# Convolution taps dealt out on VectorE's queue over retention, keys and attention, and probabilities scaled on ScalarE

## The chip, the cores and the metric

The kernel runs on one core of one Trainium2 chip. The metric is the device time of one execution in microseconds (us), from the first to the last instruction and what lies around them. A core has the engines TensorE (PE: matrix products, with a queue of its own for loading weights, PEld), VectorE (DVE), ScalarE (ACT), GpSimd (POOL) and SyncE (SP, which issues the DMAs here). Each engine works through its own queue in order.

## What is computed

A transformer block of two layers on 512 tokens of width 1024 in float32. The normed input is projected once (`w_in`), and its columns feed three branches: attention over compressed, selected and windowed keys with 8 heads in 2 groups, retention with 4 heads, and a convolution module. The branches are projected, mixed by sigmoid gates and added; a feed-forward with a squared ReLU follows. What the change touches:

```python
def _masked_softmax(s, mask):
    s = jnp.where(mask, s, -1e30)
    m = jnp.max(s, axis=-1, keepdims=True)
    p = jnp.exp(s - m) * mask
    den = jnp.sum(p, axis=-1, keepdims=True)
    return p / jnp.maximum(den, 1e-30)

def _conv_module(a, b, dw_w, dw_b, ln_g, ln_b):
    u = a * jax.nn.sigmoid(b)
    kern = dw_w[:, None, :].astype(u.dtype)
    y = lax.conv_general_dilated(u, kern, window_strides=(1,), padding=[(CONV_WIDTH - 1, 0)],
                                 dimension_numbers=('NWC', 'WIO', 'NWC'), feature_group_count=CONV_CH)
    y = y + dw_b
    y = _layernorm(y, ln_g, ln_b)
    return jax.nn.silu(y).astype(a.dtype)
...
        gs = jax.nn.sigmoid(gb.astype(jnp.float32)).reshape(B, Q_BLOCK, G, HPG, 3)
        o = gs[..., 0:1] * o_c + gs[..., 1:2] * o_s + gs[..., 2:3] * o_w
```

The convolution is depthwise: 512 channels, 31 taps each, over the tokens.

## The kernel before

Every product of two matrices is made in three: each operand is split into a high part and the remainder, and the products high by high, high by low and low by high are added up in PSUM (`proj`, L156). Weights are streamed from HBM by SP into `wr` (three buffers); ACT makes the high part `wh` (L144), POOL the low part `wl` in two halves (L147; in the feed-forward DVE does, L149). Activations are split by `split` (L110): ACT copies the high part (L111), DVE subtracts (L112). Tokens lie along the free axis, 512 wide, channels along the 128 partitions, so most tiles are 128x512.

A scheduler orders each engine's queue by a simulated timeline of its own: of the instructions whose inputs it takes to be there it puts the first in program order. `tc.issue_after(i)` adds one constraint: what is written inside it stands behind instruction `i` on `i`'s engine.

A layer runs like this. The normed input X is split (`norm_split`). `conv_input` (L303) makes one of four blocks of 128 channels of the convolution's input `u`, the first ahead of the retention, the others after its heads. The depthwise convolution is 31 taps for each of 4 channel blocks, 124 in a layer; each is one DVE instruction on 128x512 (the first of a block L331, the others L333) that multiplies a shifted view of `u` by a column of weights and adds it into `yc`. They stand in a list `todo`, and `conv_taps(n)` (L324) writes the next `n` where it is called, if their `u` has been written. It is called with 2 after each of 8 rotations (`T_ROT`, L362), with 1 after each of 16 score splits of the retention (`T_SCORE`, L418), with 2 after each of 64 pieces in attention (`T_QUERY`, L722), and for the rest at L748. As nothing holds a tap back but its input and the tap before it, those taps that are called for in retention suffice, with what the scheduler pulls forward, to place all 124 ahead of the first query.

The retention of a head computes scores on PE, multiplies them by the decay on DVE (L416), splits them (L111, L112) and forms the product with the values in the PSUM tile `av` (L108 is every product's line). Then the keys follow: `compress` (L481) lays blocks of tokens out (`XP`, L496) and projects them to the compressed keys and values; other projections are split into the attention's keys (L558) and values (L567), and the first query is projected (`query`, L636; its DVE step `tq` is L641).

Attention has 16 blocks in a layer: 4 turns `j`, 2 groups `g`, 2 branches `br`, each of one head. A block: scores of 4 pieces of 128, 256, 384 and 512 columns in the PSUM tile `sc`, bias and maximum on DVE (L705), exponential and denominator on ACT (L706), the gate over the denominator (`gate_over`, L617, three small DVE operations), and then for each piece

```python
nc.vector.tensor_scalar(cols[i], cols[i], c[:, i:i + 1], None, op0=OP.mult)
pt = ps("tp")
for k in range(i + 1):
    nc.tensor.transpose(pt[:, k * P:(k + 1) * P], cols[i][:, k * P:(k + 1) * P], ident)
```

(L712 to L715), the split of the transposed piece by ACT (L720) and DVE (L721), and at the block's end eight products with the values into `av`. PE's order interleaves this with fillers, pieces of work that are ready long before: the projection of the retention's output mixed with a gate, and gates ahead of time (`fill`, L470; their DVE step is `g`, L444). 19 of 24 fillers are dealt over the 16 blocks, each behind the first score product of a block (L743, L744); the others come after attention. Once all taps are written, `conv_norm` (L578) normalises the convolution in four steps between the blocks. PSUM has 3 banks for `mm`, 2 for `sc`, 2 for `tp` and 1 for `av`.

## Time and profile before

| | |
|---|---|
| runs of the kernel before | 1836.65, 1838.71, 1839.05 us (median 1838.71) |
| the profiled execution | 1835.35 us |
| its span, first to last instruction | 1833.6 us |
| mean granted TensorE clock over the span | 0.983 |

The page of the profile gives each engine's busy time over the span, which averages over stages with different limits. The span in slices and tables of stretches show the stages apart: retention and keys, attention, mixing and feed-forward, twice. Lines of waits say which engine waited for which tile, and how long; groups by shape give one instruction's mean time. The granted clock is the share of full speed at which TensorE was let run.

### The profile page before, as it was taken

The numbers are of one execution on the slowest core, as the hardware profiler recorded it, in microseconds if no ns is written. First come the engines' busy times: TensorE is split into PE (matmuls) and PEld (weight loads), VectorE is DVE, ScalarE is ACT, GpSimd is POOL, SyncE is SP. The second block draws the span as 40 slices with busy tenths as digits, with TensorE's granted clock in tenths as the row PEclk, the third lists the DMA queues.
The fourth block names the chain that finished last, engine by engine and source line by source line (L and its number), as shares of the span: only waits on it lengthen the run. The fifth ranks groups of instructions, "written<-read, shape, count | busy, mean of one in ns | idle before, by whom it ended". The sixth has DMA issues, their size and how long they took to land.

```text
span 1833.6 us, 23278 instructions
## 1 busy us (share of the span) xinstructions
PE 1759.7 (96%) x8592; PEld 1474.4 (80%) x8592; DVE 1162.1 (63%) x2107; ACT 721.4 (39%) x1293; POOL 512.0 (28%) x420
## 2 busy tenths in 40 slices
PE   8899899999999999999999878999999999999997
PEld 7777788888888888888897767888888888888886
DVE  7999977777554343434479998767766443434344
ACT  4423445566343232323433324555653432313231
POOL 4444433423471000000344544343235700000000
PEclk9999999999999999999999989999999999999998
DMA  4221442322653223233422113233128432232221
GB/s 165 83 74 59 130 150 94 113 87 81 229 167 104 92 92 103 92 94 102 144 81 75 65 58 129 98 110 109 69 81 268 141 97 92 93 103 92 94 91 69
DMA packets 70801, 195.82 MB, mean 107 GB/s; under 512 B 8944, under 2 KB 9328, under 8 KB 70688
## 3 DMA queue, kind: packets, MB, share of 16 engines
q1 hardware_dynamic: 70688, 194.34, 32.2%
q8 instruction: 68, 1.11, 0.2%
q14 instruction: 45, 0.37, 0.1%
HBM read 177.51 MB, written 19.42 MB: 107 GB/s over the span
## 4 chain that ended last, share of the span: by engine, by line
PE 58%; issue 21%; DVE 20%; DMA 1%; ACT 0%; SPq 0%; POOLq 0%; POOL 0%; DVEq 0%; ACTq 0%
PE mm L108 50%; DVE yc L333 9%; PE sc L108 3%; PE av L108 2%; PE tp L715 2%; DVE pr L112 1%; PE tp L108 1%; DVE rt L416 1%; DVE kv L558 1%; DVE qk L381 1%; DVE rr L359 0%; DVE t L395 0%; DVE XP L496 0%; DMA m<-in_cmp_w_k_dram 0%; DVE rr L360 0%
## 5 line engine op out<-in xcount | busy, mean ns | idle before, releaser
L108 PE MATMUL mm<-X,wh 128*128 128x512 f32 x2432 | 772.8, 396 | 17.4 <-ACT X L213 6.2
L147 POOL TENSOR_TENSOR wl<-wr,wh 128x512 fp32r<-128x512 f32 (+2 forms) x344 | 442.2, 1308 | 530.4 <-ACT wh L144 478.9
L144 ACT ACTIVATE wh<-wr 128x1024 fp32r<-128x1024 f32 (+2 forms) x301 | 296.4, 986 | 658.7 <-PE mm L108 554.1
L108 PEld LDWEIGHTS mm<-X,wh 128*128 128x128 f32 x2432 | 455.1, 190 | 108.3 <-ACT X L213 6.2
L108 PE MATMUL mm<-X,wl 128*128 128x512 f32 x1216 | 480.7, 395 | 0.2 <-DVE wl L149 0.2
L108 PEld LDWEIGHTS mm<-X,wl 128*128 128x128 f32 x1216 | 230.6, 190 | 46.8 <-DVE wl L149 0.6
L333 DVE SCALAR_TENSOR_TENSOR yc<-u,ccol,yc 128x512 f32<-128x512 f32 x240 | 227.5, 960 | 1.9
L149 DVE TENSOR_TENSOR wl<-wr,wh 128x1024 fp32r<-128x1024 f32 x129 | 158.1, 1225 | 38.6 <-ACT wh L144 38.6
L108 PE MATMUL mm<-bo,wh 128*128 128x512 f32 x512 | 163.5, 397 | 6.3 <-DVE g L444 5.8
L108 PE MATMUL mm<-fa,wh 128*128 128x512 f32 x512 | 160.2, 395 | 0.0
L796 DVE SCALAR_TENSOR_TENSOR t<-mm,rs 128x512 f32<-128x512 f32 x64 | 43.9, 691 | 161.3 <-PE mm L108 156.0
L205 POOL TENSOR_TENSOR n<-n,mhalf 128x4 f32<-128x4 f32 x15 | 18.1, 1208 | 403.8 <-DVE n L203 403.8
L226 POOL TENSOR_TENSOR t<-t,t 128x512 f32<-128x512 f32 x18 | 27.4, 1524 | 333.6 <-DVE wl L149 314.4
L108 PE MATMUL mm<-kv,wh 128*128 128x512 f32 x384 | 119.5, 389 | 0.0
L108 PEld LDWEIGHTS mm<-bo,wh 128*128 128x128 f32 x512 | 97.5, 191 | 26.8 <-DVE g L444 6.2
L108 PEld LDWEIGHTS mm<-fa,wh 128*128 128x128 f32 x512 | 96.1, 188 | 23.2
L721 DVE TENSOR_TENSOR pt<-tp,pt 128x256 fp32r<-128x256 f32 (+1 forms) x192 | 70.3, 373 | 55.2 <-ACT pt L720 54.7
L108 PE MATMUL mm<-bo,wl 128*128 128x512 f32 x256 | 101.2, 395 | 0.0
L108 PE MATMUL mm<-fa,wl 128*128 128x512 f32 x256 | 100.6, 395 | 0.0
L108 PE MATMUL mm<-wh,X 128*128 128x256 f32 (+1 forms) x480 | 94.5, 295 | 4.2 <-DVE t L307 4.2
L720 ACT ACTIVATE pt<-tp 128x256 fp32r<-128x256 f32 (+1 forms) x192 | 63.9, 343 | 86.0 <-PE tp L715 53.3
L807 DVE TENSOR_TENSOR yc<-yc,mm 128x512 f32<-128x512 f32 x32 | 22.0, 688 | 105.6 <-PE mm L108 105.6
(219 smaller groups left out, 2449.2 us busy)
## 6 DMA issues: line engine op xcount, KB each, us to landing
wr<-in_w_dram SPq DMA_DIRECT2D x128, 512.0 KB, 3.5
wr<-in_w_f_dram SPq DMA_DIRECT2D x87, 512.0 KB, 3.2
wr<-in_w_b_dram SPq DMA_DIRECT2D x48, 256.0 KB, 2.7
wr<-in_w_t_dram SPq DMA_DIRECT2D x16, 512.0 KB, 3.2
gd<-g SPq DMA_DIRECT2D x32, 256.0 KB, 2.0
g<-gd SPq DMA_DIRECT2D x32, 256.0 KB, 3.3
wr<-in_w_o_dram SPq DMA_DIRECT2D x16, 512.0 KB, 3.6
md<-g SPq DMA_DIRECT2D x16, 256.0 KB, 2.6
```

Of the source, the lines that this page charges most:

```text
L108: return nc.tensor.matmul(o, l, r, start=start, stop=stop)
L112: (eng or nc.vector).tensor_sub(lo, src, f(hi))
L144: nc.scalar.activation(h, t, AF.Copy)
L147: nc.gpsimd.tensor_sub(l[:, k], t[:, k], f(h[:, k]))
L149: nc.vector.tensor_sub(l, t, f(h))
L226: (nc.vector if c == KC - 1 or first_time else nc.gpsimd).tensor_add(s, s, acc)
L333: nc.vector.scalar_tensor_tensor(yc[c], x, w, yc[c], op0=OP.mult, op1=OP.add)
L715: nc.tensor.transpose(pt[:, k * P:(k + 1) * P], cols[i][:, k * P:(k + 1) * P], ident)
L720: nc.scalar.activation(vh, src, AF.Copy)
L721: nc.vector.tensor_sub(vl, src, f(vh))
L796: nc.vector.scalar_tensor_tensor(t, pf, 0.0, rs, op0=OP.max, op1=OP.mult)
L807: nc.vector.tensor_add(xT[m], xT[m], pf)
```

## The change

The two calls that deal taps in the retention are given other numbers (1 after each rotation, 2 after each score split), and new ones stand in the keys (3 after each of the 4 layings-out of L496 and after each of the 2 key splits, 6 after the values). Whatever is then left of `todo` is counted (`late_taps`) and dealt evenly over the first 52 of attention's 64 pieces. Each call is now `conv_taps_behind`, which puts the taps on DVE's queue behind the operation that it follows, so that the scheduler no longer takes them forward. For that, `split` returns its subtraction. The scaling of the probabilities by the gate over the denominator, 128 instructions in all, goes from DVE to ACT, as a copy with a scale of one value per partition.

```diff
--- before.py
+++ after.py
@@ -74,7 +74,8 @@
     count = [0]
 
 
-    T_ROT, T_SCORE, T_QUERY = 2, 1, 2
+
+    T_ROT, T_SCORE, T_KEYS, T_SLOTS = 1, 2, 3, 52
 
 
     AHEAD, F_KEYS, HELD = 16, 1, 4
@@ -109,7 +110,7 @@
 
     def split(hi, lo, src, eng=None):
         nc.scalar.activation(hi, src, AF.Copy)
-        (eng or nc.vector).tensor_sub(lo, src, f(hi))
+        return (eng or nc.vector).tensor_sub(lo, src, f(hi))
 
     def halves(g):
 
@@ -315,6 +316,10 @@
             nc.gpsimd.memset(u[:, :CW - 1], 0.0)
             nc.vector.scalar_tensor_tensor(u[:, CW - 1:], tb, 1.0, ta, op0=OP.add, op1=OP.mult)
             us.append(u)
+
+        def conv_taps_behind(ins, n):
+            with tc.issue_after(ins.ins):
+                conv_taps(n)
 
         conv_input(0)
         yc = [tl(cp, "yc", 4) for _ in range(4)]
@@ -357,9 +362,9 @@
                 nc.vector.tensor_mul(B[:, :, 0, :], z[:, :, 1, :], sinb)
                 nc.vector.tensor_mul(B[:, :, 1, :], z[:, :, 0, :], sinb)
                 nc.vector.tensor_sub(A[:, :, 0, :], A[:, :, 0, :], B[:, :, 0, :])
-                nc.vector.tensor_add(A[:, :, 1, :], A[:, :, 1, :], B[:, :, 1, :])
+                rotated = nc.vector.tensor_add(A[:, :, 1, :], A[:, :, 1, :], B[:, :, 1, :])
                 rr.append(A)
-                conv_taps(T_ROT)
+                conv_taps_behind(rotated, T_ROT)
             for c in range(2):
                 pt = ps("tp")
                 for i in range(NB):
@@ -414,8 +419,7 @@
                 mm(s[:, :n], KSr[h][:, j * P:(j + 1) * P], QLr[h][:, j * P:], False, True)
                 t = tl(rp, "rt", 2)
                 nc.vector.tensor_mul(t[:, :n], s[:, :n], dec[:, :n])
-                split(ph[:, at[j]], pl[:, at[j]], t[:, :n])
-                conv_taps(T_SCORE)
+                conv_taps_behind(split(ph[:, at[j]], pl[:, at[j]], t[:, :n]), T_SCORE)
             o = ps("av")
             for j in range(NB):
                 mm(o[:, j * P:], VHr[j][:, h % 2, :], ph[:, at[j]], j == 0, False)
@@ -493,7 +497,8 @@
             pe = par(pe_at, 16)
             for g in range(2):
                 blocks = bass.AP(tensor=E.tensor, offset=E.offset + g * T, ap=[list(E.ap[0]), [2, 16], [16, NCMP]])
-                nc.vector.tensor_add(XP[:, :, g, :], blocks, pe[:, :, None].to_broadcast([P, 16, NCMP]))
+                laid = nc.vector.tensor_add(XP[:, :, g, :], blocks, pe[:, :, None].to_broadcast([P, 16, NCMP]))
+                conv_taps_behind(laid, T_KEYS)
             w1t = []
             for u in range(2):
                 t = tl(rp, "w1", 4, (P, 8, P))
@@ -555,7 +560,8 @@
                 nc.scalar.activation(KHH[br, g][nat], t[nat], AF.Copy)
                 nc.scalar.activation(KHH[br, g][oth], t[nat], AF.Copy)
                 for half in (nat, oth):
-                    nc.vector.tensor_sub(KLL[br, g][half], t[nat], f(KHH[br, g][nat]))
+                    low = nc.vector.tensor_sub(KLL[br, g][half], t[nat], f(KHH[br, g][nat]))
+            conv_taps_behind(low, T_KEYS)
         G = tl(mix_pool, "G", 1, (P, NB, 24))
         V = []
         pz = [ps(tag) for tag in ("mm", "mm", "mm", "av")]
@@ -564,10 +570,11 @@
             v = kv((P, 4, P))
             zv = pz[i][:, :256].rearrange("p (c d) -> p c d", d=DH)
             nc.scalar.activation(v[:, :, 0:64], zv, AF.Copy, scale=rs4[:, i:i + 1])
-            nc.vector.scalar_tensor_tensor(v[:, :, 64:128], zv, rs4[:, i:i + 1], f(v[:, :, 0:64]), op0=OP.mult,
-                                           op1=OP.subtract)
+            low = nc.vector.scalar_tensor_tensor(v[:, :, 64:128], zv, rs4[:, i:i + 1], f(v[:, :, 0:64]), op0=OP.mult,
+                                                 op1=OP.subtract)
             nc.scalar.activation(G[:, i, :], pz[i][:, 256:280], AF.Tanh, scale=rs4h[:, i:i + 1])
             V.append(v)
+        conv_taps_behind(low, 2 * T_KEYS)
         phase.close()
 
         def ut(dtype=F):
@@ -709,7 +716,7 @@
                     c = gate_over(den, h, 1 + br)
                     ph, pl = tl(ap, "pt", 4, (P, 1280), FR), tl(ap, "pt", 4, (P, 1280), FR)
                     for i in range(NB):
-                        nc.vector.tensor_scalar(cols[i], cols[i], c[:, i:i + 1], None, op0=OP.mult)
+                        nc.scalar.activation(cols[i], cols[i], AF.Copy, scale=c[:, i:i + 1])
                         pt = ps("tp")
                         for k in range(i + 1):
                             nc.tensor.transpose(pt[:, k * P:(k + 1) * P], cols[i][:, k * P:(k + 1) * P], ident)
@@ -718,8 +725,9 @@
                             if len(vh.shape) == 3:
                                 src = src.rearrange("p (k q) -> p k q", q=P)
                             nc.scalar.activation(vh, src, AF.Copy)
-                            nc.vector.tensor_sub(vl, src, f(vh))
-                        conv_taps(T_QUERY)
+                            low = nc.vector.tensor_sub(vl, src, f(vh))
+                        slot = 4 * (4 * j + 2 * g + br) + i
+                        conv_taps_behind(low, late_taps * (slot + 1) // T_SLOTS - late_taps * slot // T_SLOTS)
                     for k, c0 in enumerate((0, 512, 896, 1152)):
                         n = T - k * P
                         lhs = V[k][:, 2 * br + g, :]
@@ -732,6 +740,7 @@
             return oj
 
         ON, marks, tqs = [], [], [query(0)]
+        late_taps = len(todo)
 
         def more(j, k):
```

What this does to the queues is shown at three places of layer 0. Names are those of the tiles with a running number; `yc` is a sum of the convolution, `u` its input, L333 before is L338 now, L112 is L113, and L721 is L728.

On DVE's queue, at the end of the first retention head's scores and in the convolution input that follows (`rt` decayed scores, `pr` their low part, `t` and `u` of the input, `n` small sums), there stood before

```order
L112 TENSOR_TENSOR pr_817<-rt_837,pr_816 128x256
L333 SCALAR_TENSOR_TENSOR yc_260<-u_257,ccol,yc_260 128x512
L112 TENSOR_TENSOR pr_817<-rt_845,pr_816 128x128
L333 SCALAR_TENSOR_TENSOR yc_260<-u_257,ccol,yc_260 128x512 x5
L307 TENSOR_TENSOR t_920<-mm_888,rs_179 128x512
L313 TENSOR_TENSOR t_954<-mm_887,rs_179 128x512
L333 SCALAR_TENSOR_TENSOR yc_260<-u_257,ccol,yc_260 128x512
L316 SCALAR_TENSOR_TENSOR u_956<-t_920,t_954 128x512
L333 SCALAR_TENSOR_TENSOR yc_260<-u_257,ccol,yc_260 128x512
L331 TENSOR_SCALAR yc_261<-u_956,ccol,pcol 128x512
L333 SCALAR_TENSOR_TENSOR yc_261<-u_956,ccol,yc_261 128x512
L402 TENSOR_TENSOR t_991<-mm_959,rs_179 128x512
```

and stands now

```order
L113 TENSOR_TENSOR pr_809<-rt_831,pr_808 128x256
L338 SCALAR_TENSOR_TENSOR yc_260<-u_257,ccol,yc_260 128x512
L113 TENSOR_TENSOR pr_809<-rt_840,pr_808 128x128
L338 SCALAR_TENSOR_TENSOR yc_260<-u_257,ccol,yc_260 128x512 x3
L308 TENSOR_TENSOR t_916<-mm_884,rs_179 128x512
L314 TENSOR_TENSOR t_950<-mm_883,rs_179 128x512
L317 SCALAR_TENSOR_TENSOR u_952<-t_916,t_950 128x512
L407 TENSOR_TENSOR t_987<-mm_955,rs_179 128x512
L204 TENSOR_SCALAR n_868<-tp_863 128x4
L421 TENSOR_TENSOR rt_999<-sc_996,dec_992 128x512
```

From the head's last split (the second L112, now L113) to the next head's gate (L402, now L407), 9 taps stood, and 3 stand now.

At the second head's last two pieces it now reads, with the two taps that stand between the third split and the last product with the decay:

```order
L421 TENSOR_TENSOR rt_1017<-sc_1014,dec_992 128x256
L338 SCALAR_TENSOR_TENSOR yc_260<-u_257,ccol,yc_260 128x512
L113 TENSOR_TENSOR pr_995<-rt_1017,pr_994 128x256
L338 SCALAR_TENSOR_TENSOR yc_260<-u_257,ccol,yc_260 128x512 x2
L432 TENSOR_TENSOR rt_859<-rt_859,tp_872 128x512
L421 TENSOR_TENSOR rt_1026<-sc_1023,dec_992 128x128
L433 SCALAR_TENSOR_TENSOR rt_859<-rt_859,pcol,gs_803 128x512
L113 TENSOR_TENSOR pr_995<-rt_1026,pr_994 128x128
```

That place is the same as it was.

On DVE's queue, from the last layings-out or value splits (`kv`) to the first query (`tq`; `m` and `kc` are of the compressed keys), there stood before

```order
L333 SCALAR_TENSOR_TENSOR yc_263<-u_1472,ccol,yc_263 128x512
L507 TENSOR_SCALAR m_1673<-m_1673 128x62
L582 TENSOR_TENSOR u_3902<-yc_262,yc_263 128x512
L567 SCALAR_TENSOR_TENSOR kv_2054<-av_1924,n_177,kv_2054 128x4x64
L508 TENSOR_TENSOR m_1673<-m_1673,tp_1656 128x62
L583 TENSOR_TENSOR u_3901<-u_3901,u_3902 128x512
L512 SCALAR_TENSOR_TENSOR m_1678<-m_1673,tp_1656 128x62
L520 TENSOR_SCALAR kc_1685<-tp_1683 64x31
L521 TENSOR_SCALAR kc_1685<-tp_1683 64x31
L641 SCALAR_TENSOR_TENSOR tq_2097<-mm_2072,rs_179 128x512
```

and stands now

```order
L573 SCALAR_TENSOR_TENSOR kv_2080<-av_1950,n_177,kv_2080 128x4x64
L336 TENSOR_SCALAR yc_262<-u_1138,ccol,pcol 128x512
L338 SCALAR_TENSOR_TENSOR yc_261<-u_952,ccol,yc_261 128x512
L338 SCALAR_TENSOR_TENSOR yc_262<-u_1138,ccol,yc_262 128x512
L338 SCALAR_TENSOR_TENSOR yc_261<-u_952,ccol,yc_261 128x512 x7
L525 TENSOR_SCALAR kc_1699<-tp_1697 64x31
L526 TENSOR_SCALAR kc_1699<-tp_1697 64x31
L338 SCALAR_TENSOR_TENSOR yc_261<-u_952,ccol,yc_261 128x512 x4
L648 SCALAR_TENSOR_TENSOR tq_2129<-mm_2104,rs_179 128x512
```

Before, the last tap of the layer stands just ahead of this place; now runs of ten and of four taps stand between the last value split and the query.

On DVE's queue, in the last third of attention, where PE's queue has its longest piece without fillers (`pt` low parts of the transposed probabilities, `tp` the transposes, `s` probabilities, `n` small, `on` the attention's output), there stood before

```order
L721 TENSOR_TENSOR pt_3858<-tp_3884,pt_3857 128x2x128
L590 TENSOR_TENSOR yc_263<-yc_263,mm_4075 128x512
L712 TENSOR_SCALAR s_4003<-s_4003,n_4024 128x128
L712 TENSOR_SCALAR s_4003<-s_4003,n_4024 128x256
L712 TENSOR_SCALAR s_4003<-s_4003,n_4024 128x384
L712 TENSOR_SCALAR s_4003<-s_4003,n_4024 128x512
L721 TENSOR_TENSOR pt_3858<-tp_3875,pt_3857 128x128
L594 TENSOR_TENSOR u_4084<-u_4084,u_4081 128x512
L721 TENSOR_TENSOR pt_3858<-tp_3884,pt_3857 128x256
```

and stands now

```order
L338 SCALAR_TENSOR_TENSOR yc_263<-u_1476,ccol,yc_263 128x512
L629 SCALAR_TENSOR_TENSOR n_4127<-G_1946,n_4127 128x4
L338 SCALAR_TENSOR_TENSOR yc_263<-u_1476,ccol,yc_263 128x512
L728 TENSOR_TENSOR pt_3852<-tp_3868,pt_3851 128x2x128
L728 TENSOR_TENSOR pt_3852<-tp_3878,pt_3851 128x2x128
L728 TENSOR_TENSOR pt_3852<-tp_3868,pt_3851 128x128
L338 SCALAR_TENSOR_TENSOR yc_263<-u_1476,ccol,yc_263 128x512
L728 TENSOR_TENSOR pt_3852<-tp_3878,pt_3851 128x256
L338 SCALAR_TENSOR_TENSOR yc_263<-u_1476,ccol,yc_263 128x512
L739 TENSOR_TENSOR on_3423<-t_3932,av_3679 64x512
L728 TENSOR_TENSOR pt_4019<-tp_4021,pt_4018 128x128
```

The four scalings have gone, and a tap stands behind each piece's splits. On PE's queue the end of the same piece reads now

```order
L109 MATMUL av_3989<-pt_4018,kv_2080 128x128
L109 MATMUL av_3989<-pt_4019,kv_2080 128x128
L722 MATMUL tp_4139<-ident,s_4106 128x128 x2
L722 MATMUL tp_4145<-ident,s_4106 128x128 x3
L722 MATMUL tp_4154<-ident,s_4106 128x128 x4
L109 MATMUL mm_4172<-ones,u_4063 128x1 x4
L109 MATMUL av_3989<-pt_4131,kv_2068 128x512
L109 MATMUL av_3989<-pt_4132,kv_2068 128x512
L109 MATMUL av_3989<-pt_4131,kv_2072 128x384
L109 MATMUL av_3989<-pt_4132,kv_2072 128x384
L190 MATMUL mm_4178<-ident,n_4171 128x128 x4
L109 MATMUL mm_4198<-X_115,wh_4201 128x512
```

From the values products of block 10 to those of block 14 no filler (`mm` from X or `bo` and `wh`, as in the last row) stands on PE's queue: 98 products, of which 14 have 512 columns, 12 have 384, 12 have 256 and 60 are of 128 columns or fewer. The longest such piece before has 61 products.

## Rows read from the trace of the kernel before

**Rows 1.** The page: busy time of each engine, share of the span, instructions.
```profile
PE 1759.7 (96%) x8592; PEld 1474.4 (80%) x8592; DVE 1162.1 (63%) x2107; ACT 721.4 (39%) x1293; POOL 512.0 (28%) x420
```

**Rows 2.** The page: the span in 40 slices of 45.8 us, busy share in tenths.
```profile
DVE  7999977777554343434479998767766443434344
```

**Rows 3.** Stretches: length, busy PE, PEld, DVE, ACT, POOL, granted clock, DMA share, GB/s.
```profile
40.00:242.00 202.00, 179.66 (x977) 153.68 (x975) 194.55 (x283) 71.53 (x118) 97.99 (x70) 0.95 0.29 97
242.00:470.00 228.00, 225.35 (x1173) 190.53 (x1172) 163.90 (x502) 129.95 (x320) 75.37 (x68) 0.99 0.28 96
930.00:1144.00 214.00, 186.01 (x1061) 162.16 (x1060) 203.39 (x302) 72.36 (x120) 97.67 (x67) 0.94 0.24 81
1144.00:1376.00 232.00, 229.85 (x1190) 194.30 (x1189) 164.43 (x501) 131.19 (x321) 79.01 (x70) 0.99 0.28 95
```

**Rows 4.** Stretches, taps alone: length, busy DVE (instructions), clock, DMA share, GB/s.
```profile
40.00:242.00 202.00, 108.11 (x115) 0.95 0.29 97
...
930.00:1144.00 214.00, 115.66 (x120) 0.94 0.24 81
```

**Rows 5.** PE's waits, 40 to 242, 930 to 1144, 242 to 470: total us, times, longest.
```profile
PE av L108 <- DVE pr L112: 8.7, 6, 3.4
...
PE av L108 <- DVE pr L112: 8.3, 4, 5.0
PE mm L108 <- ACT G L569: 5.9, 1, 5.9
...
PE av L108 <- DVE pt L721: 1.6, 1, 1.6
```

**Rows 6.** Timeline at 180 to 202 us: start, length, engine, line, operation, tiles, count.
```profile
182.26 6.94 POOL L147 TENSOR_TENSOR wl<-wr,wh 128x512 fp32r<-128x512 f32 x4 [6.68 <-ACT wh L144]
...
183.36 3.45 DVE L333 SCALAR_TENSOR_TENSOR yc<-u,ccol,yc 128x512 f32<-128x512 f32 x2
...
196.38 5.09 DVE L333 SCALAR_TENSOR_TENSOR yc<-u,ccol,yc 128x512 f32<-128x512 f32 x7
```

**Rows 7.** Chain of waits in a feed-forward, and timeline at 236 to 244 us.
```profile
578.15 343.62 PE mm L108 x1504
...
239.06 3.74 PE L108 MATMUL tp<-XP,w 128*128 128x62 f32 x32
```

**Rows 8.** Groups of POOL, 40 to 242 and 242 to 470 us: busy, mean ns, idle before.
```profile
L147 POOL TENSOR_TENSOR wl<-wr,wh 128x512 fp32r<-128x512 f32 x48 | 73.6, 1557 | 71.5 <-ACT wh L144 64.9 <-PE tp L108 3.7 <-issue 2.8
...
L147 POOL TENSOR_TENSOR wl<-wr,wh 128x512 fp32r<-128x512 f32 x47 | 61.9, 1339 | 107.2 <-ACT wh L144 100.0 <-PE tp L715 3.6 <-PE sc L108 1.9
```

**Rows 9.** Groups of DVE by shape, whole span.
```profile
L721 DVE TENSOR_TENSOR pt<-tp,pt 128x256 fp32r<-128x256 f32 x128 | 52.7, 418 | 29.2 <-ACT pt L720 28.9
L712 DVE TENSOR_SCALAR s<-s,n 128x512 f32<-128x512 f32 x32 | 22.4, 701 | 0.0
L712 DVE TENSOR_SCALAR s<-s,n 128x384 f32<-128x384 f32 x32 | 19.5, 608 | 0.0
L721 DVE TENSOR_TENSOR pt<-tp,pt 128x128 fp32r<-128x128 f32 x64 | 18.2, 285 | 26.0 <-ACT pt L720 25.8
L705 DVE CUSTOM_DVE_ANT_0 s<-sc,bias 128x512 f32<-128x512 f32 x32 | 22.0, 687 | 14.1 <-PE sc L108 13.9
L712 DVE TENSOR_SCALAR s<-s,n 128x256 f32<-128x256 f32 x32 | 13.2, 412 | 0.0
L712 DVE TENSOR_SCALAR s<-s,n 128x128 f32<-128x128 f32 x32 | 9.0, 282 | 0.6
```

**Rows 10.** Stretch of the piece without fillers in attention, columns as in rows 3.
```profile
396.00:408.00 12.00, 10.25 (x58) 8.34 (x57) 11.07 (x50) 6.91 (x24) 1.92 (x2) 0.86 0.19 68
```

**Rows 11.** Groups of ACT by shape, whole span.
```profile
L111 ACT ACTIVATE fa<-t 128x512 fp32r<-128x512 f32 x32 | 19.8, 630 | 0.8
L213 ACT ACTIVATE X<-on,pcol 128x512 fp32r<-128x512 f32 x12 | 8.5, 709 | 0.1
```

## The prediction

> **What bounds the kernel now.** The first view is the page's busy times: TensorE (PE) is busy for 96% of the span, VectorE (DVE) for 63% [rows 1]. Read alone that says that moving DVE's work gains nothing. The page's slices correct it: DVE is at 90% or more in the slices from 46 to 229 us and again from 963 to 1100, and at 30 to 40% in the feed-forward that lies between [rows 2]. So the second view is the table of stretches. The retention and keys of layer 0 lie about between 40 and 242 us, of layer 1 between 930 and 1144; attention follows each [rows 3]. In the first kind DVE is busy for 194.55 of 202.00 us and 203.39 of 214.00: it sets the pace there. PE is idle for 202.00 − 179.66 = 22.3 and 214.00 − 186.01 = 28.0 us, and its granted clock has a mean of 0.95 and 0.94. In attention the roles are turned: PE is busy 225.35 of 228.00 us, DVE 163.90.
>
> The third view asks what DVE does in the first kind: the taps alone take 108.11 and 115.66 us [rows 4], over half of it. The fourth view is PE's waits: nearly all long ones there end with DVE (the split of the decayed scores, L112, 8.7 us in 6 waits and 8.3 in 4) or with something that DVE held up (the G of L569, which waits in a PSUM bank for DVE to empty the one before, 5.9 us) [rows 5]. In attention PE's waits are about nothing: 1.6 us is the largest [rows 5]. A tap costs 0.73 us when nothing disturbs it (5.09 us for 7), but two of them took 3.45 us beside a weight split on GpSimd (POOL), whose four took 6.94 [rows 6].
>
> **The change, part by part.** All sums are made against the profiled execution, 1835.35 us (span 1833.6); the median of the runs is 1838.71, so 3.4 us are added at the end.
>
> *Taps that leave the front.* Before, all 124 taps of a layer stand on DVE's queue ahead of the queries. The order after has 8 in the rotation, 32 in the scores and 24 by the keys, values and the query: 64, and 60 are left for attention. Their price: 108.11 over 115 recorded is 0.94 us, 115.66 over 120 is 0.96 [rows 4], so 60 × 0.95 = 57 us of DVE's work leave each first stage. DVE then has 194.6 − 57 = 138 and 203.4 − 57 = 146 us of work, PE 180 and 186 at the clock it had: PE becomes the bound. What can come back is at most PE's idle time, 22.3 + 28.0 = 50.3, and its clock, (1 − 0.95) × 202 + (1 − 0.94) × 214 = 10.1 + 12.8 = 22.9: 73.2 us over both layers.
>
> I do not take all of it. The order still puts two taps between a head's last score product and the split that the values product waits for (as at the second head's last two pieces, which read as before), 2 × 0.73 = 1.4 us at each of 4 heads, 5.6 a layer; and in layer 0 the last values' split is followed by 10 taps, then 4 more after the two keys, then the query. That run is 14 × 0.73 plus a few small operations, 11 to 15 us; PE has beside it some 48 products of 512 columns at 343.62/1504 = 0.228 us and 17 narrow ones at 3.74/32 = 0.12 [rows 7], 13 us: I count 2.5 us lost. So 2 × 5.6 + 2.5 = 14 us of waits stay, and a quarter of the clock's 22.9, 6 us, with them. The step gives 73.2 − 14 − 6 = **53 us**.
>
> *Taps that enter attention.* 60 taps cost DVE there 60 × 0.73 = 44 undisturbed and 57 at the price that they had in the front; I take 52, since POOL's splits are there too, but fewer and shorter, 1.34 us against 1.56 [rows 8]. Out go the scalings of the probabilities: a block's four pieces take 0.70 + 0.61 + 0.41 + 0.28 = 2.00 us [rows 9], 16 blocks 32 us. DVE goes from 163.9 to 163.9 + 52 − 32 = 184 of 228 us, 81%. By its share it still fits; by its place on the chain of a block it need not. A block runs scores, maximum, exponential, scaling, transposes, split, product; the taps stand behind each split (L721, 0.42 and 0.29 us [rows 9]) and so ahead of the next one.
>
> PE hides that by fillers, gate and mix projections that need nothing of DVE's chain. The order shows where they fail: from the values product of block 10 to that of block 14, PE's queue has 98 products and no filler; the longest such piece before has 61. The 98 take 14 × 0.228 + 12 × 0.171 + 12 × 0.114 + 60 × 0.12 = 14 us. On DVE's queue stand in the same piece 17 taps (17 × 0.73 = 12.4), 24 splits (16 × 0.42 + 8 × 0.29 = 9.0), two blocks' score additions at about the scalings' prices (0.69 for the widest [rows 9]; 3.9) and some 26 small ones, about 4 with their overlaps: 29 us. DVE comes into it with a lead that I put at 4 us, so PE waits 29 − 14 − 4 = 11. Today the same place costs 12.00 − 10.25 = 1.75 us of idle time and 12.00 × (1 − 0.86) = 1.7 of clock [rows 10], 3.4 together. That is 8 us more in each layer. For the other blocks I add 3 a layer: each has a filler, but the splits come later by the taps between them. **22 us** are lost.
>
> *The scaling on ScalarE (ACT).* The trace has no such instruction. The nearest are a copy with a factor of one value per partition, 0.71 us at 128x512, and plain splits, 0.63 [rows 11]; DVE's own is 0.70 [rows 9]. By their ratios to DVE's 0.70 a block's four would be 1.8 to 2.0 us against 2.00; on the chain of 32 blocks that is between −6 us, if nothing hid it, and nothing. I take zero, since PE's fillers hide the chain where they stand. ACT goes from 129.95 to about 162 of 228 us in attention and still has room. It also frees DVE from waiting behind the denominators' small operations.
>
> A rule speaks against the taps' new place. What the row shows first: beside POOL's split a pair of taps took 3.45 instead of 1.46 us, and POOL's own pieces are slower in the front (1.56) than in attention (1.34) [rows 6, 8], so whoever of the two is there makes the other wait. The Trainium skill (SBUF — State Buffer, "SBUF: two separate sides") says that a VectorE operation with two inputs in SBUF and a GpSimd operation share one pair of ports as an exclusive lock, so that the loser is blocked for the whole instruction. The trace agrees with it by those rows; by the rule the fillers' weight splits would slow down in attention as they speed up in the front, a rival below.
>
> *Sum.* −53 + 22 = −31; 1835.35 − 31 = 1804.4, and 3.4 for the runs: **1808 us**.
>
> **The rivals.** *Attention takes the taps for nothing.* DVE is idle there for 64 us a layer [rows 3], and the splits could be early enough. Against it stands the piece without fillers. Then only residues of the front are lost: −60, **1779 us**.
>
> *The front does not give back what it should.* Its waits could be chains through PSUM and ACT that DVE's load merely shares: the wait on L569's G is named ACT's [rows 5]. Half the gain, −26, and attention's 22: −4, **1835 us**, at the edge of what can be told from no change.
>
> *Slower: attention's fillers fail in most blocks.* One block without cover costs (29 − 14)/4 = 3.8 us, and there are 32. With the front's −53 the change turns to a loss from 14 such blocks; the order shows about 8. If half of them are bare, because a tap behind a split always comes before the next split and the fillers' own gate operations (L444) wait behind taps too, 16 × 3.8 = 62: +9, **1848 us**. All 32 would be +70.
>
> *The port rule.* Taps beside POOL's splits make filler weights late: 60 taps a layer that each hold up a split by 0.2 us (the difference of the two means) are 24 us over both, 20 of them on the path: −53 + 22 + 20 = −11, **1828 us**.
>
> That the change does not move the taps is excluded: the order shows them.
>
> **Chances.** The forecast with its own range, 1795 to 1825, has 0.53; attention for nothing 0.20; the front's half gain 0.11; slower 0.10; ports 0.06. About 0.2% (3.7 us) is what a measurement can tell from no change. Faster: 0.53 + 0.20 + 0.05 of the ports + 0.04 of the half gain = 0.82; the same: 0.06 + 0.01 = 0.07; slower: 0.10 + 0.01 = 0.11. The range from 1772 to 1835 leaves out the slower case, half of the half gain and a little of the best: 0.2.
>
> **What would show it.** Right: in the two fronts DVE's busy share falls from 96 to about 80%, PE's idle time from 50 to under 20 us, the clock goes above 0.97; in attention DVE is busy 180 to 190 us a layer, a new wait of PE on the split after the transposes stands at the piece without fillers, about 10 us, with a lower clock; ACT's scalings are 0.4 to 0.7 us. Wrong: if attention stalls in many blocks rather than in one place (then slower), if PE still idles in the front with DVE at 80% (the half gain), if POOL's splits in attention become as long as in the front, or if a scaling on ACT costs over 0.8 us.

## The result and the profile after

The changed kernel takes 1804.51 us (median of 4 runs, 1803.38 to 1806.04), the kernel before 1838.51 beside it. The ratio is 0.9817 (95% interval 0.98 to 0.9834): 34 us less, with 1808 forecast in a range from 1772 to 1835. The profiled execution's span fell from 1833.6 to 1803.0 us, by 30.6.

The page after, with its busy times and VectorE's slices, is to be set beside [rows 1, 2]:

```profile
span 1803.0 us, 23260 instructions
PE 1757.3 (97%) x8592; PEld 1473.8 (82%) x8592; DVE 1104.4 (61%) x1979; ACT 774.9 (43%) x1421; POOL 500.6 (28%) x420
...
DVE  6976978887554344434459778878857443434344
```

TensorE's share has gone up by one point and VectorE's down by two; the slices at 90% or more, seven before, are three. What moved where is told by stretches. I cut both kernels at the same three events of a layer: the rotation's first operation, the first query's step on VectorE (L641, now L648), and the end of the last block of attention; the third stretch is the mixing up to the feed-forward. Columns are those of [rows 3], first of the kernel after, the three stretches of layer 0 and then the first two of layer 1:

```profile
29.50:220.70 191.20, 181.60 (x1061) 159.56 (x1060) 152.73 (x238) 73.06 (x121) 87.56 (x69) 0.97 0.32 103
220.70:457.00 236.30, 228.86 (x1157) 190.98 (x1157) 187.24 (x503) 157.82 (x386) 80.43 (x66) 0.97 0.28 92
457.00:570.10 113.10, 113.10 (x502) 92.95 (x501) 58.89 (x71) 40.62 (x58) 61.63 (x53) 1.00 0.56 181
923.60:1104.70 181.10, 178.26 (x1058) 159.61 (x1057) 146.46 (x237) 71.50 (x120) 87.26 (x69) 0.98 0.29 95
1104.70:1340.80 236.10, 228.95 (x1153) 191.01 (x1152) 187.08 (x500) 157.34 (x384) 80.37 (x66) 0.96 0.28 90
```

and of the kernel before, the first two of each layer:

```profile
29.50:239.70 210.20, 187.86 (x1044) 161.88 (x1043) 202.03 (x301) 73.83 (x121) 97.30 (x69) 0.95 0.28 92
239.70:471.60 231.90, 229.25 (x1201) 194.18 (x1201) 165.36 (x505) 131.21 (x323) 77.67 (x69) 0.99 0.29 98
...
932.40:1143.60 211.20, 183.21 (x1039) 159.44 (x1038) 200.80 (x298) 71.33 (x119) 97.67 (x67) 0.94 0.23 79
1143.60:1377.30 233.70, 231.55 (x1197) 195.66 (x1197) 165.46 (x502) 132.84 (x324) 79.01 (x70) 0.99 0.29 96
```

Read each line in two ways: length less busy PE is idle time, and length by what the clock lacks of 1.00 is an estimate of the time lost to the clock (the clock is read to two places, so each such term is good to about 1 us). In retention and keys idle time goes from 22.3 and 28.0 to 9.6 and 2.8 us, 38 less, and the clock's share from 10.5 and 12.7 to 5.7 and 3.6, 14 less: 52 together. In attention idle time goes from 2.7 and 2.2 to 7.4 and 7.2, 10 more, and the clock's from 2.3 and 2.3 to 7.1 and 9.4, 12 more: 22 together. 52 − 22 = 30, which is near the span's difference of 30.6. (Attention looks only 4 and 2 us longer, since some products now run later, in the mixing: in layer 0 it has 502 products in 113.1 us, before 476 in 107.2, at full clock both times.) VectorE is busy for 80% and 81% of the two fronts, 96% and 95% before, and for 79% of attention, 71% before.

The taps alone, in retention and keys and then in attention of layer 0, are to be set beside [rows 4]:

```profile
29.50:220.70 191.20, 54.72 (x61) 0.97 0.32 103
220.70:457.00 236.30, 50.56 (x59) 0.97 0.28 92
```

50.56 us over 59 recorded is 0.86 us for a tap in attention, 54.72 over 61 is 0.90 in front. PE's waits in the front of layer 0 (the front is retention and keys), then around the stretch of PE's queue that has no fillers (376 to 412; it is called the bare piece below), then the only wait on DVE in the front of layer 1, are to be set beside [rows 5]:

```profile
PE mm L109 <- ACT G L575: 4.7, 1, 4.7
PE av L109 <- DVE pr L113: 2.8, 2, 1.8
PE tp L371 <- DVE rr L365: 2.1, 2, 1.5
...
PE av L109 <- ACT pt L727: 2.3, 4, 0.7
PE tp L722 <- DVE pt L728: 1.9, 2, 1.5
PE sc L109 <- DVE n L712: 1.8, 2, 1.6
PE av L109 <- DVE on L739: 0.7, 1, 0.7
PE av L109 <- DVE pt L728: 0.3, 1, 0.3
...
PE tp L371 <- DVE rr L365: 0.5, 1, 0.5
```

And the stretches of attention in layer 0: ahead of the bare piece, the piece with a little on either side, behind it, and the same piece of layer 1 (compare [rows 10]):

```profile
220.70:378.00 157.30, 156.89 (x811) 132.65 (x811) 127.72 (x356) 108.51 (x268) 61.86 (x51) 1.00 0.32 104
376.00:412.00 36.00, 28.98 (x131) 21.95 (x130) 31.86 (x92) 21.81 (x63) 3.81 (x3) 0.81 0.14 45
412.00:457.00 45.00, 45.00 (x227) 38.03 (x226) 29.58 (x63) 29.50 (x64) 15.94 (x13) 1.00 0.25 81
1260.00:1296.00 36.00, 29.25 (x130) 22.39 (x129) 31.65 (x89) 21.14 (x62) 3.06 (x3) 0.76 0.15 45
```

Nearly all of attention's loss is in one place. Ahead of the piece PE is busy for 156.89 of 157.30 us at clock 1.00, behind it for all of 45. In the piece it idles 7.0 us, in ten waits of at most 1.6, and loses 0.19 × 36 = 6.8 by the clock; in layer 1 it is 6.8 and 8.6. From the last filler ahead of it to the first one behind it the bare piece is 31.1 us long in layer 0 (381.2 to 412.3); before, it is 13.7 (394.2 to 407.9).

### The profile page after: what moved, and what is told of

It is laid out like the page before. It is cut to its first block, busy times and chain, and to the rows that moved or that the text cites. A ratio compares the mean times of both kernels' runs of the same rounds, so it can differ in the third digit from the quotient of the medians.

```text
span 1803.0 us, 23260 instructions
## 1 busy us (share of the span) xinstructions
PE 1757.3 (97%) x8592; PEld 1473.8 (82%) x8592; DVE 1104.4 (61%) x1979; ACT 774.9 (43%) x1421; POOL 500.6 (28%) x420
## 4 chain that ended last, share of the span: by engine, by line
PE 67%; issue 20%; DVE 10%; ACT 2%; DMA 1%; SPq 0%; POOLq 0%; POOL 0%; DVEq 0%; ACTq 0%
PE mm L109 58%; PE sc L109 3%; DVE yc L338 3%; PE av L109 3%; PE tp L722 2%; PE tp L109 1%; DVE XP L500 1%; DVE kv L563 1%; DVE qk L386 1%; ACT s L719 0%; DVE pt L728 0%; ACT wh L145 0%; DVE rr L364 0%; PE tp L190 0%; DVE s L712 0%
## 5 line engine op out<-in xcount | busy, mean ns | idle before, releaser
L148 POOL TENSOR_TENSOR wl<-wr,wh 128x512 fp32r<-128x512 f32 (+2 forms) x344 | 436.2, 1290 | 563.2 <-ACT wh L145 540.6
L338 DVE SCALAR_TENSOR_TENSOR yc<-u,ccol,yc 128x512 f32<-128x512 f32 x240 | 214.2, 894 | 1.7
L109 PEld LDWEIGHTS mm<-fa,wh 128*128 128x128 f32 x512 | 96.1, 188 | 23.2
L714 ACT ACTIVATE s<-s,n 128x128 f32<-128x128 f32 (+3 forms) x128 | 71.4, 559 | 46.9 <-DVE n L712 46.3
L109 PE MATMUL mm<-wh,X 128*128 128x256 f32 (+1 forms) x480 | 90.1, 286 | 0.0
L728 DVE TENSOR_TENSOR pt<-tp,pt 128x128 fp32r<-128x128 f32 (+1 forms) x192 | 70.0, 372 | 32.7 <-ACT pt L727 32.4
```

The lines of the kernel that those rows point to most:

```text
L109: return nc.tensor.matmul(o, l, r, start=start, stop=stop)
L148: nc.gpsimd.tensor_sub(l[:, k], t[:, k], f(h[:, k]))
L338: nc.vector.scalar_tensor_tensor(yc[c], x, w, yc[c], op0=OP.mult, op1=OP.add)
L714: nc.scalar.activation(s, s, AF.Exp, scale=-1.0, bias=mx[:, i:i + 1], accum_out=den[:, i:i + 1])
L728: low = nc.vector.tensor_sub(vl, src, f(vh))
```

## The experiments

Eight undo or shift one part, four put parts together. Times are medians beside runs of the kernel before on the same chip, ratios are to those.

**Scalings back on VectorE.**

```diff
-nc.scalar.activation(cols[i], cols[i], AF.Copy, scale=c[:, i:i + 1])
+nc.vector.tensor_scalar(cols[i], cols[i], c[:, i:i + 1], None, op0=OP.mult)
```

> The changed kernel with the 128 scalings back on VectorE, nothing else. If the prediction is right that VectorE's load matters only in the piece of attention without fillers, this adds two blocks' scalings there, 2 x 2.0 us a layer, and is otherwise hidden: 1804.5 + 8 = 1812 us. If the scaling is what makes room for the taps (32 us of VectorE's work a layer), attention stalls in more places: 1820 us or more. If the scaling costs on ScalarE as much as it saves on VectorE (four pieces take 2.2 us there against 2.0): 1802 to 1806 us.

1802.79 us, ratio 0.9795 (0.9775 to 0.9815); the changed kernel's was 0.9817 (0.98 to 0.9834). The two can't be told apart, so in this arrangement the scaling's place is worth nothing. The prediction's account, by which VectorE's work in the bare piece is what counts, gave 1812 and missed: two blocks' scalings more on VectorE there, about 4 us a layer, cost nothing. The row of attention in layer 0 shows that VectorE is fuller and PE none the worse, against 228.86 of 236.30 above:

```profile
221.50:458.10 236.60, 230.77 (x1162) 193.15 (x1162) 205.17 (x567) 129.36 (x322) 79.84 (x66) 0.96 0.28 93
```

**Only the scalings moved, in the kernel before.**

```diff
-nc.vector.tensor_scalar(cols[i], cols[i], c[:, i:i + 1], None, op0=OP.mult)
+nc.scalar.activation(cols[i], cols[i], AF.Copy, scale=c[:, i:i + 1])
```

> The kernel before with only the 128 scalings moved to ScalarE; taps as before. If the scaling is worth nothing by itself (attention is TensorE's, fillers hide the chain), the time stays within 3 us of the kernel before. If it relieves VectorE where attention waits for it, 4 to 8 us less. The run without ordering, which has it too, was 4 us above the kernel before on the same chip; if the scaling is what made it so, 3 to 6 us more here.

Ratio 1.0015 (0.9995 to 1.0035): nothing, as expected.

**No ordering behind an operation.**

```diff
-            with tc.issue_after(ins.ins):
-                conv_taps(n)
+            conv_taps(n)
```

> The changed kernel without the ordering behind an operation: the same calls with the same numbers, but the scheduler may take the taps forward as in the kernel before. If what gives the time is that taps leave the retention and the keys, nearly all of it goes: the front is VectorE's again, attention is free of taps and has the scalings on ScalarE: 1830 to 1840 us. If the new numbers alone (1, 2, 3 in place of 2, 1) do it, it stays at 1805.

Ratio 1.0024 (1.0009 to 1.0038): the whole gain is gone, and with these numbers the kernel is a trace slower than before (1843.86 us, a little above the 1830 to 1840 expected). The front of layer 0 is VectorE's again, 201.96 of 210.60 us as in the kernel before:

```profile
29.70:240.30 210.60, 187.70 (x1044) 161.74 (x1043) 201.96 (x300) 73.82 (x121) 97.28 (x69) 0.95 0.29 92
```

So the new numbers do nothing where the scheduler may take taps forward; holding them back is the change.

**Attention's taps left out.**

```diff
-        late_taps = len(todo)
+        todo[:] = [(c, k) for c, k in todo if k == 0]
+        conv_taps(len(todo))
+        late_taps = 0
...
-            if not todo:
+            if 4 * j + k >= 12:
```

> The changed kernel with the taps of attention left out (59 or 60 a layer; the sums of the last two channel blocks are then incomplete), and the convolution's normalisation written at the same four blocks as before. If the taps are what stalls TensorE in attention, both layers lose the 21 us of stalls that attention has gained: about 1784 us, with no long wait in the piece without fillers. If the stalls come from the scaling on ScalarE and its place on the chain, they stay: 1800 us or more.

1786.4 us, ratio 0.9711 (0.9688 to 0.9735): 18 less than with them. That is the price of 118 taps in attention, 59 a layer (without them the convolution's sums are incomplete), and the scaling on ScalarE, which stays in this kernel, has no part in it:

```profile
220.60:456.40 235.80, 230.74 (x1189) 193.85 (x1188) 142.43 (x446) 158.89 (x389) 78.88 (x70) 0.99 0.30 99
```

The bare piece of layer 0 is 9.5 us long here (383.5 to 393.0), against 31.1 with the taps.

**The normalisation behind attention.**

```diff
-            if not todo:
-                next(normed, None)
```

> The changed kernel with the normalisation of the convolution written behind attention instead of between its last blocks; the taps and scalings stay. Theory one: the piece is without fillers because its fillers are used up by their pacing, and the normalisation has nothing to do with it: 1803 to 1807 us. Theory two: the fillers are held back because the normalisation's column sums, which wait for the last taps, take banks of the fillers' PSUM tile in between; then fillers stand in the piece, its stalls of 19 us a layer go down to under half, and the time to 1785 to 1795 us, unless the normalisation is exposed at the end of attention, which would show as a wait there.

1811.52 us, ratio 0.9845 (0.9823 to 0.9866): 7 more by the medians, 5 by the ratios, whose intervals just overlap; above what either theory gave. The rows of the bare piece's old place and of what follows it, in layer 0:

```profile
376.00:420.00 44.00, 39.95 (x205) 33.01 (x204) 32.49 (x91) 28.19 (x72) 12.12 (x9) 1.00 0.25 85
420.00:446.00 26.00, 20.51 (x91) 17.15 (x91) 18.97 (x48) 13.35 (x36) 3.64 (x3) 0.74 0.07 21
```

The second theory is right in its mechanism: with the normalisation gone from there, fillers stand in the old place, at clock 1.00. That it is by its PSUM banks, and not by another rule of the scheduler, was not tried apart. And the bare piece has moved to where the normalisation now stands (420.0 to 443.1; 26.00 − 20.51 = 5.5 us idle, clock 0.74), at the end of attention. The changed kernel's own timeline shows the same order at the end of its bare piece:

```profile
405.30 1.89 PE L109 MATMUL av<-pt,kv 128*128 128x512 f32 x4 [0.47 <-ACT pt L727]
...
405.82 0.74 DVE L338 SCALAR_TENSOR_TENSOR yc<-u,ccol,yc 128x512 f32<-128x512 f32 x1
406.81 1.53 DVE L338 SCALAR_TENSOR_TENSOR yc<-u,ccol,yc 128x512 f32<-128x512 f32 x2
...
408.46 0.68 DVE L589 TENSOR_TENSOR u<-yc,yc 128x512 f32<-128x512 f32 x1
...
410.13 1.05 PE L109 MATMUL mm<-ones,u 128*128 128x1 f32 x8
...
411.95 0.60 PE L190 MATMUL mm<-ident,n 128*128 128x128 f32 x4
...
412.31 0.71 PE L109 MATMUL mm<-X,wh 128*128 128x512 f32 x2
```

The last taps come late (405.82, 406.81), then the additions over the four sums (L589 at 408.46, L590 at 409.40), then the column sums on PE (410.13) and the row transposes (411.95), all in the `mm` banks, and with the next row, 412.31, the fillers resume. The four products of 1.89 us, 0.47 each, run at the lower clock level, against 0.228 [rows 7].

**Late taps over 40 pieces instead of 52.** In program order the last tap then stands two blocks ahead of the normalisation.

```diff
-    T_ROT, T_SCORE, T_KEYS, T_SLOTS = 1, 2, 3, 52
+    T_ROT, T_SCORE, T_KEYS, T_SLOTS = 1, 2, 3, 40
...
-            if not todo:
+            if 4 * j + k >= 12:
```

> The changed kernel with the late taps dealt over 40 of attention's pieces instead of 52, so that the last stands in block 9, and the normalisation of the convolution written from block 12 on, as in the changed kernel. Theory: the 18 us that attention costs come from taps and normalisation meeting in the one piece where the fillers are held back; the earlier blocks, all covered by fillers, take 1.5 taps a piece for nothing. Then about 1787 us, as with the late taps left out. Rival: VectorE's load in attention costs wherever it is put, by late splits: 1803 us or more, with new waits of TensorE in blocks 0 to 9.

1797.2 us, ratio 0.9777 (0.976 to 0.9795): 7 less than the changed kernel, 11 more than with the taps left out, and between the 1787 and the 1803 that the two theories gave. By its median it is the fastest complete kernel of this study. Ending the dealing earlier takes back 7 of the 18 us; 11 stay. The trace shows where part of them are: the bare piece is shorter, 14.1 us (382.0 to 396.1), but the last two taps still run in it, at 386.78 and 387.77, with L589 behind them at 389.43. Its row in layer 0,

```profile
380.00:396.00 16.00, 13.68 (x69) 11.29 (x68) 14.20 (x52) 12.05 (x34) 2.56 (x2) 0.79 0.15 50
```

has 2.3 us of idle time and 3.4 of clock.

**No taps behind the layings-out; and none behind the values.** Two runs:

```diff
-                conv_taps_behind(laid, T_KEYS)
```

```diff
-        conv_taps_behind(low, 2 * T_KEYS)
+        conv_taps_behind(low, 0)
```

> The changed kernel without taps behind the four layings-out of the compressed keys and values; those 12 a layer go to attention with the others (72 in place of 60). In layer 0 TensorE waits 4.7 us for the gates' column that ScalarE reads (L575), and ScalarE waited 4.9 us before it on a small operation that stands on VectorE's queue behind the layings-out and their taps. If these taps make that wait, it goes, layer 0's retention and keys become 4 to 7 us shorter with the clock, and attention pays some 2 to 4 us a layer for 12 more taps: 1798 to 1806 us. If the layings-out themselves make it, retention and keys stay within 2 us and the time rises to 1808 to 1812.

> The changed kernel without the six taps behind the values; they go to attention (66 in place of 60). The prediction counted 2.5 us lost in layer 0 by the run of taps between the last value split and the query. If so, retention and keys of layer 0 get 2 to 3 us shorter, and attention 1 to 2 us longer in each layer: 1803 to 1806 us. If the run costs nothing (TensorE has enough beside it), only attention's part shows: 1806 to 1809 us.

Without those behind the layings-out 1804.36 us (0.9816, 0.9797 to 0.9835), without those behind the values 1807.75 (0.9834, 0.9819 to 0.9849). The first takes the 4.7 us wait on G in layer 0 down to 0.7:

```profile
PE mm L109 <- ACT G L574: 0.7, 1, 0.7
```

yet the time stays, as if attention paid it back for 12 more taps; that was not followed stage by stage. In the second that wait stays (4.7 us), so the run of taps behind the values is not what made it.

**Together.** Over 40 pieces with the scalings on VectorE (60 taps a layer, 1.5 a piece of attention); the same without taps behind the layings-out (72 taps, 1.8 a piece); that over 32 pieces, normalisation from block 10 (2.25 a piece); and the second with the scalings on ScalarE. The edits are those above, but for

```diff
-    T_ROT, T_SCORE, T_KEYS, T_SLOTS = 1, 2, 3, 40
+    T_ROT, T_SCORE, T_KEYS, T_SLOTS = 1, 2, 3, 32
...
-            if 4 * j + k >= 12:
+            if 4 * j + k >= 10:
```

> The run with the late taps over 40 pieces, with the scalings back on VectorE. The single undoing of the scaling gave 1802.8 against 1804.5 for the changed kernel. If its value is on the chain of a bare block alone (2.2 us for four pieces on ScalarE, 2.0 on VectorE), the same 0 to 3 us come off 1797.2: 1794 to 1797. If VectorE is now fuller in blocks 0 to 9, where the taps are denser, the scaling has its use there: 1800 or more.

> The same, and without taps behind the four layings-out (72 in attention's first 40 pieces). The single move gave 6 us less in layer 0's retention and keys and as much more in attention, where the taps met the normalisation. Here attention's end is free of them: 4 us come off retention and keys, 2 are paid in the covered blocks: 1791 to 1796. If 72 taps in 40 pieces (1.8 a piece) are too many for VectorE's chain, 1799 or more.

> The same again, with the taps over 32 pieces (2.25 a piece) and the normalisation from block 10 on, so that the piece of TensorE's queue without fillers is the shortest of all (47 products). If the piece without fillers is what costs, 2 to 6 us less than over 40 pieces. If the density of taps is, more than over 40 pieces by as much.

> Late taps over 40 pieces, none behind the layings-out (72 a layer in attention), the scalings on ScalarE. With the scalings on VectorE the same placing gave 1808.9 us, and the step from VectorE to ScalarE was worth 16.7 us with 60 taps in these 40 pieces. If VectorE's fullness in the covered blocks is what the scaling buys off, it is worth as much or more with 72 taps: 1790 to 1795 us, a few less than with 60 taps (1797.2), since layer 0's retention and keys are 6 us shorter. If 1.8 taps a piece fill VectorE even without the scalings, the gain in front is paid back in attention: 1797 to 1802 us.

They gave 1813.91 (0.9857, 0.9841 to 0.9873), 1808.89 (0.9834, 0.9819 to 0.9849), 1835.93 (0.998, 0.9968 to 0.9992) and 1806.41 us (0.9818, 0.9792 to 0.9844). I had expected 1794 to 1797, 1791 to 1796, 2 to 6 less again, and 1790 to 1795: four misses, all to the side that the expectations had named for a VectorE that is too full, the last two beyond what they gave for it. Three 40 us stretches of attention in layer 0, with 60 taps in 40 pieces and the scalings on ScalarE (1797.2 us),

```profile
260.00:300.00 40.00, 40.00 (x210) 33.97 (x209) 35.27 (x104) 28.68 (x72) 13.31 (x13) 1.00 0.33 102
...
340.00:380.00 40.00, 39.38 (x206) 33.24 (x206) 33.02 (x94) 29.79 (x74) 13.44 (x11) 1.00 0.36 118
380.00:420.00 40.00, 37.68 (x194) 31.70 (x193) 31.33 (x91) 28.69 (x70) 8.81 (x8) 0.91 0.18 60
```

and with them on VectorE (1813.91 us):

```profile
260.00:300.00 40.00, 40.00 (x211) 34.00 (x210) 38.55 (x107) 20.54 (x53) 15.18 (x14) 1.00 0.26 86
...
340.00:380.00 40.00, 35.12 (x166) 29.20 (x165) 35.41 (x98) 21.36 (x55) 11.70 (x9) 0.91 0.25 81
380.00:420.00 40.00, 36.18 (x194) 31.32 (x193) 36.99 (x121) 24.20 (x63) 9.83 (x7) 0.91 0.22 76
```

show it. VectorE's 38.55 of 40 us leave PE covered from 260 to 300; from 340 to 380 PE has 4.9 us of idle time and clock 0.91, where the other kernel has 0.6 and 1.00. That idle time lies in the first 10 us:

```profile
340.00:350.50 10.50, 5.62 (x30) 4.59 (x29) 10.40 (x31) 5.33 (x15) 2.49 (x2) 0.92 0.21 74
350.50:380.00 29.50, 29.50 (x137) 24.62 (x137) 25.01 (x69) 16.04 (x41) 9.21 (x7) 0.91 0.27 84
```

and from 342.3 to 350.3 no filler runs: a second bare piece, which the other kernel does not have, with VectorE busy for 10.40 of 10.50 us. PE's two waits there are both on VectorE, 3.2 us on a maximum (L712) and 1.7 on a split (L728) with a tap on either side. So the scaling that is worth nothing with 60 taps over 52 pieces (1.15 a piece) is worth 16.7 us with 1.5. With 1.8 a piece even ScalarE's help is not enough (1806.41 against 1797.2); the last run, 72 taps in 40 pieces with it, has VectorE at 38.81 of 40 us from 300 to 340 and PE's idle time there and behind:

```profile
300.00:340.00 40.00, 38.27 (x196) 31.56 (x195) 38.81 (x89) 23.11 (x56) 18.89 (x14) 1.00 0.32 107
340.00:380.00 40.00, 37.35 (x181) 31.26 (x181) 32.58 (x85) 27.51 (x68) 13.13 (x10) 0.91 0.29 95
```

Between the two runs with 72 taps the scaling makes 2.5 us, inside their intervals. Why it does so little there, after 16.7 with 60 taps, the runs leave open. Nor does VectorE's load alone put these kernels in order: with the scalings on VectorE, 72 taps gave 1808.89 us and 60 gave 1813.91, though the first query of layer 0 comes 7 us earlier in the one with 72 (213.96 against 221.11).

## Why the prediction was right

**The bound.** Retention and keys were VectorE's, and 60 taps less a layer made them TensorE's: the fronts give 52 us, where 53 were forecast. That it is the taps' leaving, and not the scaling or the numbers, is shown by the runs without ordering and with the scaling alone. Of the signs that were named, VectorE's share in the fronts (80 and 81%) and its time in attention (187 us) came as told; the clock in the front of layer 0 is 0.97 and not above it, and the new wait in the bare piece is not one of 10 us on the split after the transposes but ten short ones, 7.0 us together, of which 2.2 are on VectorE's part of that split (L728).

**The residue in front** was 14 us of waits and 6 of clock in the forecast; it is 12.4 and 9.3. The sum is near, its parts are not. The forecast kept 1.4 us at each of 8 heads, 11 in all; the first rows of waits show 2.8 at the heads of layer 0, and in layer 1 there is none on that split. The two taps ahead of a head's last split still stand there, so they did not make the waits; that the backlog of a full VectorE did is the reading that is left. For layer 0's keys 2.5 us were forecast, by the run of taps between values and query; measured are 4.7 and the clock behind it, and by the two runs the taps between the layings-out make it: ScalarE's queue waits 4.9 us for a small operation that stands behind them on VectorE's, and G, which frees the PSUM bank, stands on ScalarE behind that.

**Attention.** Forecast 22 us, measured 22, and 18 by leaving the taps out. The place was right, the sum was luck: its terms are wrong and make up for one another. The forecast placed 8 a layer in the bare piece and 3 elsewhere; nearly all of it is in the piece: 13.9 us against 3.4 before in layer 0, 15.4 against 3.6 in layer 1. Elsewhere it is about nothing. In the piece 11 us of waiting were forecast and no clock; measured are 7.0 and 6.8 of waiting, with 6.8 and 8.6 of clock. Nor is the way there borne out, VectorE's work of 29 us less PE's 14 and a lead of 4: more of VectorE's work in the same place, with the scalings back, cost nothing. The forecast read off the queue that the piece has no fillers; why was not asked. The runs show that it stands where the convolution's normalisation does, which cannot run before the last tap, and that it is the shorter the earlier the taps end: 31.1, 14.1 and 9.5 us in layer 0 with taps over 52 pieces, over 40, and left out.

**The price of a tap** in attention was taken as 52/60 = 0.87 us; it is 0.86.

**The scaling** was taken at 1.8 to 2.0 us for a block's four and as nothing in the sum. The groups of ScalarE by shape:

```profile
L719 ACT ACTIVATE s<-s,n 128x512 f32<-128x512 f32 x32 | 22.8, 713 | 0.0
L719 ACT ACTIVATE s<-s,n 128x384 f32<-128x384 f32 x32 | 19.4, 606 | 0.0
L719 ACT ACTIVATE s<-s,n 128x256 f32<-128x256 f32 x32 | 15.9, 498 | 0.0
L719 ACT ACTIVATE s<-s,n 128x128 f32<-128x128 f32 x32 | 12.8, 399 | 11.2 <-DVE n L629 11.1
```

give 0.71 + 0.61 + 0.50 + 0.40 = 2.22 us, more than the forecast's upper end and than VectorE's 2.00 [rows 9]; that it is worth nothing here was right. The forecast scaled all four pieces by the ratio at 512 columns; the narrow ones do not follow it. The Trainium skill has this (ScalarE: Activation LUTs, "What ACT_TABLE_LOAD costs"): with one operand that points to a value per partition, a bias on the page and a scale here, an activation takes about 280 ns and 0.833 ns a column. That is an estimate of 707, 600, 493 and 387 ns, and the rows agree within 13 ns. What the forecast did not see is the scaling's worth with 60 taps over 40 pieces.

**The rivals.** Attention does not take the taps for nothing (18 us by leaving them out). The front gave back what it should. Fillers fail in one piece a layer, not in half of the blocks (that rival's price was also added up a little high: 16 × 3.8 is 60.8 and not 62). But its direction is real in fuller kernels: with 1.5 taps a piece and the scalings on VectorE a second bare piece opens, as shown above. The port rule: POOL's halves of a weight split, in front and in attention of layer 0,

```profile
L148 POOL TENSOR_TENSOR wl<-wr,wh 128x512 fp32r<-128x512 f32 x45 | 63.3, 1428 | 64.8 <-ACT wh L145 64.8
...
L148 POOL TENSOR_TENSOR wl<-wr,wh 128x512 fp32r<-128x512 f32 x48 | 67.1, 1419 | 128.1 <-ACT wh L145 117.1 <-PE tp L722 5.0 <-PE sc L109 4.8
```

took 1.43 and 1.42 us, against 1.56 and 1.34 [rows 8]. The Trainium skill's rule of the shared ports (SBUF — State Buffer, "SBUF: two separate sides") fits their direction, and a tap's 0.86 us against 0.73 alone too. But PE waits for no weights there: no row of its waits names them. So this cost is not on PE's path.

## What to carry to other kernels

An engine that is at 63% over the span may be the bound of a stage and idle in another; read it by stages, and move its filler work, not its share. Work that is dealt into a covered stage must leave room on the queue that takes it: here a little over one tap a piece was hidden outside the bare piece, 1.5 only with the scalings gone from the same queue, and 1.8 in neither case. Look for the place where the cover itself waits for the work that is moved (the normalisation behind the last tap), and end the dealing well ahead of it, by the time at which the last piece runs and not by the order in the program.

## What was not expected of the hardware

A copy with one factor per partition is as dear on ScalarE as the same scaling on VectorE at 512 columns, 0.71 against 0.70 us, but not at 128, 0.40 against 0.28. And the bare piece, with ten waits of at most 1.6 us, cost about twice its idle time: in 36 us PE idled 7.0 and by the estimate above lost 6.8 more, since its granted clock, 1.00 in the stretches on both sides, fell to a mean of 0.81. It is not a fixed ratio: in the fronts before, 50.3 us of idle time came with 23.2 of clock.
